# A decoder trunk on one core: the shared values by seven products of halves, with weight sums and a copy of the input through DRAM

## The chip, the core and the metric

The kernel runs on one core of a Trainium2 chip. The core has a matrix engine (TensorE, in profiles PE, with its weight loads as PEld), a vector engine (VectorE, DVE), an activation engine (ScalarE, ACT), a general engine (GpSimd, POOL) and a synchronisation engine (SyncE, SP) which here only issues DMAs. Sixteen DMA engines move data between DRAM and the on-chip memory (SBUF); matmul results go to eight banks of 128 x 512 float32 (PSUM). The metric is the device time of one execution in microseconds (us), taken as the median of the runs.

## The reference

A trunk of two layers on x of 512 tokens by 1024 features, in float32. Layer 0 has a dilated window attention and a gated ConvFFN. After it, keys, values and forget gates are computed once from the residual stream; layer 1 has an attention that uses them, and its own ConvFFN. The part that matters here:

```python
if l == N_A:
    kvf = rms_norm(h, kv_norm) @ w_kvf                  # (512 x 1024) @ (1024 x 2064)
    k_sh = kvf[..., :B_WIDTH].reshape(B, T, B_HEADS, HEAD_DIM)
    v_sh = kvf[..., B_WIDTH:2 * B_WIDTH].reshape(B, T, B_HEADS, HEAD_DIM)
    log_f = jax.nn.log_sigmoid((kvf[..., 2 * B_WIDTH:] + b_f).astype(jnp.float32))
    c_sh = jnp.cumsum(log_f, axis=1)
mix = fox_mixer(rms_norm(h, g[0]), w_q_b[j], w_o_b[j], k_sh, v_sh, c_sh)
```

The values are X W with X of 512 x 1024 (tokens by features, normed and scaled by the key gain) and W the columns 1024 to 2047 of `w_kvf`. The queries use the same normed rows with another gain.

## The kernel before

Every float32 matrix is split into a high and a low part of the matmul's type, and each product takes three matmuls (`mm3`, L294 to L297): high by high, high by low, low by high. A weight of 128 x 1024 is a piece of the list `pieces`. The class `Weights` (L33) loads pieces in the order of the list (`load`, L44: an SP DMA into a `t4` tile), splits them (`high`, L52: ACT casts the high part; `low`, L71: DVE subtracts it and leaves the low part; `high_added` with `low_added`, L92 to L102: ACT also writes the negative, and a DMA issued by POOL adds the raw weight to it) and hands them out (`get`). `high` of piece n first loads up to piece n + 2. The instructions of each engine run in the order in which the program issues them; the engines wait for one another by data and by tile slots. There are 16 slots of 8 KB a partition (`t8`: split weights, input parts, keys, values), 10 of 4 KB (`t4`: raw weights, rows, bias, down-weight sums), 8 of 2 KB (`t2`) and 8 PSUM banks. A new tile takes the slot of one that was released, and its first write waits for the last use of that one.

The stage around the change comes between the two layers. `SharedBoundary` (L485) norms the four token blocks of 128 in the order 2, 3, 0, 1 and transposes them: `transpose` (L512) turns a block on TensorE, DVE multiplies by the key gain (`xf`, L523), ACT and DVE split it into `xkh` and `xkl` (L528, L529), and ACT keeps the unscaled copy in SBUF (`nT`, L533), from which `second` (L535) later makes the queries' input, one 128-feature row of tiles at a time (`xqh` on ACT, L539, `xql` on DVE, L540).

Then, in the order of the program: the first half of the values (columns 1024 to 1535) block by block, with the transposes of blocks 0 and 1 between them; eight key columns (`keys`, L1581: 24 matmuls of width 512, an ACT copy and a DVE subtraction each), with two rows of the queries' input behind each of the first four and one step of the forget gates (`gates`, L1592) behind keys 1 to 5; the second half of the values in four steps over all four blocks, with the first query's product between; and then the attention of layer 1, a loop over 8 pairs of heads and 4 query blocks whose softmax (`f_exp`, L1770) needs DVE, ACT, a bias loaded by SP and a mask by POOL. Each half of the values is 96 matmuls of 128 x 512.

`down_sums` (L602) goes beside it. The ConvFFN's down-projection already uses seven products, and this generator prepares the sums of its weights for layer 1, six pairs here: SP loads a pair into two `t4` tiles, four DVE subtractions (L628) form the sums one step later, and POOL stores them to DRAM (L610). Its seven steps are spread: one before the keys, two behind keys 0 and 1, four behind the steps of the second half of the values. After the values the program has 18 matmuls of query 1, the split of query 2's weight, 12 matmuls of the first scores, and the attention loop.

Of the kernel before, what the change touches and what calls it, by code (L numbers as in the profile page):

```python
# [115 lines left out]
def trunk_kernel(ctx, tc, x, norm_gains, w_qkv_a, w_o_a, w_q_b, w_o_b, kv_norm, w_kvf, b_f,  # L116
# [11 lines left out]
    def t8(shape, dt=F32, name="t8"):  # L128
        return p8.tile(shape, dt, tag="t8", name=name)
# [16 lines left out]
    def cols(w, k0, nk, c0, nc_):  # L146
        return w[k0 * 128:(k0 + nk) * 128, c0:c0 + nc_].rearrange("(k p) c -> p k c", p=128)
# [4 lines left out]
    def add(f):  # L152
        pieces.append(f)
# [19 lines left out]
    def add_cols(w, c):  # L173
        add(lambda raw, c=c: [(raw.rearrange("p (k c) -> p k c", k=8), cols(w, 0, 8, c, 128))])
# [19 lines left out]

    add_rows(w_o_a[0], range(6))
    add_ffn(0)
    for hf in range(2):
        for s in range(4):
            add(lambda raw, hf=hf, s=s: [(raw.rearrange("p (k c) -> p k c", k=2),
                                          cols(w_kvf, 2 * s, 2, 1024 + hf * 512, 512))])  # L200
            if hf == 1 and s == 0:
                add_cols(w_q_b[0], 0)
        if hf == 0:
            for c in range(8):
                add_cols(w_kvf, c * 128)
    for c in range(1, 8):
        add_cols(w_q_b[0], c * 128)
    add_rows(w_o_b[0], range(8))
# [276 lines left out]
    class SharedBoundary(Boundary):  # L485
# [26 lines left out]
        def transpose(self, b, later=None):  # L512
            if self.xT is None:
                self.xT = new_xT(self.name)
                self.nT = [t8([128, 4, T], name=f"nT{i}") for i in range(2)]
            xn, s = self.xn.pop(b), slice(b * 128, b * 128 + 128)
            pts, xfs = [], []
            for i in range(2):
                pt = bank([128, 4, 128], name="xt_ps")
                for k in range(4):  # L520
                    pe.transpose(pt[:, k, :], xn[:, (4 * i + k) * 128:(4 * i + k + 1) * 128], ident)
                xf = t2([128, 4, 128], name="xf")
                dve.tensor_tensor(xf, pt, self.gains[:, 4 * i:4 * i + 4, None].to_broadcast([128, 4, 128]), ALU.mult)  # L523
                pts.append(pt)
                xfs.append(xf)
            for i, xf in enumerate(xfs):
                hi, lo = self.xT[0][i][:, :, s], self.xT[1][i][:, :, s]
                act.copy(hi, xf)  # L528
                dve.tensor_tensor(lo, xf, hi.bitcast(F32), ALU.subtract)  # L529
            if later is not None:  # L530
                later()
            for i, pt in enumerate(pts):
                act.copy(self.nT[i][:, :, s], pt)  # L533

        def second(self, xT, kc):  # L535

            n, g = self.nT[kc // 4][:, kc % 4, :], self.gains[:, 8 + kc:9 + kc]
# [101 lines left out]
    def in_two():  # L639
        return [t4([128, 1024], name="dsums") for _ in range(2)]  # L640
# [937 lines left out]

    kst = {}

    def keys(c):  # L1581
        o = bank([128, T], name="k_ps")
        feat_mm(W.get(), bd2.xT, o, ALL)
# [3 lines left out]
        act.copy(k[:, 0], o)  # L1587
        dve.tensor_tensor(k[:, 1], o, k[:, 0].bitcast(F32), ALU.subtract)

    c8 = t2([16, T], name="c8")  # L1590

# [32 lines left out]
        yield  # L1624


    Vt = {}

    def values(banks, w, s, blocks):
        for b in blocks:  # L1630
            for k in range(2):
                kc = 2 * s + k
                ah, al = xs(bd2.xT, kc, slice(b * 128, b * 128 + 128))
                mm3(banks[b], ah, al, w[0][:, k, :], w[1][:, k, :], kc == 0, kc == KD - 1)

    def value_weight():
        return [t.rearrange("p (k c) -> p k c", k=2) for t in W.get()]

    def keep_values(hf, b, o):
        if hf not in Vt:  # L1640
            Vt[hf] = t8([128, 4, 512], name=f"Vt{hf}")
        (act.copy if b % 2 else dve.tensor_copy)(Vt[hf][:, b, :], o)

    down1 = down_sums([(1, j) for j in range(6)], in_two, pool, 1, 0)
    first, second = bd2.order[:2], bd2.order[2:]
    gate = gates()
    banks = {b: bank([128, 512], name="v_ps") for b in bd2.order}
    wv = []
    W.ahead = 1
    for sp_, b in [(sp_, b) for b in bd2.order for sp_ in (0, 2)]:  # L1650
        if len(wv) < 4:
            wv += [value_weight(), value_weight()]
        for s in (sp_, sp_ + 1):
            values(banks, wv[s], s, (b,))
        if (sp_, b) == (0, first[1]):
            bd2.transpose(second[0], lambda: bd2.norm(second[1]))
        if (sp_, b) == (0, second[0]):
            bd2.transpose(second[1])
            W.ahead = 3
        if b in second:  # L1660
            W.split(min(W.n_split + 1, W.n_get + W.ahead))
            if sp_ == 2:
                for bb in (first[second.index(b)], b):
                    keep_values(0, bb, banks[bb])
    del wv
    next(down1)

    bia = {}

    def load_bias(n):  # L1670
# [34 lines left out]


    xTq = [], []
    for c in range(8):
        keys(c)
        for kc in range(2 * c, min(2 * c + 2, KD)):  # L1710
            if kc % 4 == 0:
                for part, name in zip(xTq, ("xqh", "xql")):
                    part.append(t8([128, 4, T], F32R, name=f"{name}{kc // 4}"))
            bd2.second(xTq, kc)
        if 1 <= c <= 5:
            next(gate)
        if c in (0, 1):
            next(down1)
        if c == 6:
# [6 lines left out]
    banks = [bank([128, 512], name="v_ps") for _ in range(4)]  # L1726
    for s in range(4):
        values(banks, value_weight(), s, range(4))
        next(down1, None)
        if s == 0:  # L1730
            W.ahead = 2
            q_part(0, 0)
            q_part(0, 1)
            load_bias(0)
        elif s == 1:
            q_part(0, 2)
            load_bias(1)
        elif s == 2:
            q_part(0, 3)
            q_high(0)  # L1740
            q_low(0)
            load_bias(2)
    for b in range(4):
        keep_values(1, b, banks[b])


    prob = {}
# [212 lines left out]
```

## Time and profile before

| | us |
|---|---|
| median of 3 runs (1090.96 to 1092.12) | 1091.28 |
| profiled execution, its own time | 1093.78 |
| its span | 1092.0 |
| first half of the values | 509.9 to 533.3 |
| keys and gates | 533.3 to 580.7 |
| second half of the values, with query 0 | 580.7 to 607.9, and a part of query 1 behind it to 612.1 |

The profile is of one execution. Times of the lower rows are counted from the span's start. A group of instructions is given with its line, engine, operation, output and inputs, its count and its mean duration; a timeline row gives start and duration, and in brackets the idle time before it with what ended it. Matmuls are pipelined, so that one lasts longer than the distance to the next.

### The profile page before, as it was taken

To read this page: it belongs to the slowest core of one execution; us is meant where nothing else is said; L and a number is where in the kernel's file an instruction comes from. 1 tells how busy PE (TensorE), PEld (TensorE's weight loads), DVE (VectorE), ACT (ScalarE), POOL (GpSimd) and SP (SyncE) were. 2 spreads that over 40 slices of the span, in tenths; PEclk is the share of its full clock that TensorE was granted. 3 is DMA by queue.
4 is the path that set the end of the run, shared out by engine and by line. 5 is a ranking of instruction groups with operands and counts; after the bars stand their busy time and mean duration, and the time that the engine had idled before them with its cause. 6 is when DMAs were issued, how large, how long until landed. Compare 5 with 4: busy or idle time off the path is not lost.

```text
span 1092.0 us, 18966 instructions
## 1 busy us (share of the span) xinstructions
PE 1080.9 (99%) x6897; PEld 956.8 (88%) x6897; DVE 890.7 (82%) x1450; ACT 694.5 (64%) x1147; POOL 312.0 (29%) x330
## 2 busy tenths in 40 slices
PE   9999999999999999999999999999999999999997
PEld 7888889899999987888888888789899999987886
DVE  4898978679899889997686667868678899889995
ACT  6745666766775756576551587756667677746573
POOL 2643000364665532000001212000355565531000
PEclk9999999999999999999999999999999999999999
DMA  9799855898789978893447757774898878977972
GB/s 288 232 363 412 346 145 151 176 222 215 205 200 225 257 248 280 293 343 97 152 135 254 266 170 205 245 240 130 171 229 192 229 194 206 247 267 257 342 251 77
DMA packets 161525, 250.05 MB, mean 229 GB/s; under 512 B 13088, under 2 KB 106648, under 8 KB 161432
## 3 DMA queue, kind: packets, MB, share of 16 engines
q1 hardware_dynamic: 143784, 189.33, 52.2%
q0 software_dynamic: 16960, 59.52, 24.7%
q8 instruction: 54, 0.88, 0.3%
q14 instruction: 39, 0.32, 0.1%
q10 hardware_dynamic: 688, 0.01, 0.0%
HBM read 172.37 MB, written 39.73 MB: 194 GB/s over the span
## 4 chain that ended last, share of the span: by engine, by line
PE 88%; DMA 3%; DVE 3%; issue 2%; ACT 2%; SPq 1%; POOL 0%; DVEq 0%; ACTq 0%; POOLq 0%
PE up L297 12%; PE up L295 12%; PE up L296 12%; PE acc L297 8%; PE acc L295 8%; PE acc L296 8%; PE v_ps L295 2%; PE v_ps L296 2%; PE v_ps L297 2%; DVE w L831 2%; PE pT_ps L1801 1%; PE first L295 1%; PE qk_ps L295 1%; PE first L296 1%; PE first L297 1%
## 5 line engine op out<-in xcount | busy, mean ns | idle before, releaser
L295 PE MATMUL up<-xsh,w 128*128 128x256 f32 x512 | 144.9, 283 | 0.0
L296 PE MATMUL up<-xsl,w 128*128 128x256 f32 x512 | 144.9, 283 | 0.0
L297 PE MATMUL up<-xsh,w 128*128 128x256 f32 x512 | 144.9, 283 | 0.0
L736 ACT CAST w<-wraw 128x1024 fp32r<-128x1024 f32 x94 | 95.3, 1042 | 65.1 <-DVE wraw L764 44.8
L664 DVE SCALAR_TENSOR_TENSOR bb<-up,conv,bb 128x511 f32<-128x511 f32 (+1 forms) x160 | 118.3, 746 | 19.6 <-ACT bb L670 16.2
L297 PE MATMUL acc<-w 128*128 128x512 f32 (+1 forms) x311 | 120.6, 388 | 1.6 <-DVE w L831 1.6
L295 PE MATMUL acc<-w 128*128 128x512 f32 (+1 forms) x311 | 120.7, 388 | 0.5 <-DVE bb L664 0.5
L686 POOL TENSOR_TENSOR hc<-bb 128x512 f32<-128x512 f32 x44 | 77.8, 1768 | 90.5 <-DVE bb L664 60.2
L296 PE MATMUL acc<-w 128*128 128x512 f32 (+1 forms) x267 | 103.3, 387 | 0.0
L295 PEld LDWEIGHTS up<-xsh,w 128*128 128x128 f32 x512 | 98.3, 192 | 0.0
L296 PEld LDWEIGHTS up<-xsl,w 128*128 128x128 f32 x512 | 98.3, 192 | 0.0
L297 PEld LDWEIGHTS up<-xsh,w 128*128 128x128 f32 x512 | 98.3, 192 | 0.0
L296 PE MATMUL up<-xcl,w 128*128 128x256 f32 (+1 forms) x256 | 79.3, 310 | 0.0
L296 PE MATMUL up<-xbl,w 128*128 128x256 f32 (+1 forms) x256 | 79.3, 310 | 0.0
L295 PE MATMUL up<-xbh,w 128*128 128x256 f32 (+1 forms) x256 | 79.2, 310 | 0.0
L295 PE MATMUL up<-xch,w 128*128 128x256 f32 (+1 forms) x256 | 79.2, 310 | 0.0
L297 PE MATMUL up<-xbh,w 128*128 128x256 f32 (+1 forms) x256 | 79.2, 310 | 0.0
L297 PE MATMUL up<-xch,w 128*128 128x256 f32 (+1 forms) x256 | 79.2, 310 | 0.0
L76 DVE TENSOR_TENSOR w<-wraw,w 128x1024 fp32r<-128x1024 f32 x50 | 60.1, 1221 | 17.6 <-ACT w L58 13.3
L58 ACT CAST w<-wraw 128x1024 fp32r<-128x1024 f32 x61 | 62.7, 1057 | 17.9 <-DMA dsums<-in_w_down_dram 6.9
L297 PEld LDWEIGHTS acc<-w 128*128 128x128 f32 x311 | 58.4, 188 | 14.4 <-DVE w L831 2.5
L295 PEld LDWEIGHTS acc<-w 128*128 128x128 f32 x311 | 58.4, 188 | 12.8 <-ACT bb L689 0.9
(312 smaller groups left out, 3171.6 us busy)
## 6 DMA issues: line engine op xcount, KB each, us to landing
wraw<-in_w_up_dram SPq DMA_DIRECT2D x88, 512.0 KB
w<-wraw POOLq DMA_DIRECT2D x62, 512.0 KB, 5.1
dT<-dsums SPq DMA_DIRECT2D x28, 512.0 KB
dsums<-in_w_down_dram SPq DMA_DIRECT2D x22, 512.0 KB
dsums<-in_w_down_dram SPq DMA_DIRECT2D x44, 256.0 KB
hD<-hc POOLq DMA_DIRECT2D x44, 256.0 KB, 6.1
dact<-hD SPq DMA_DIRECT2D x44, 256.0 KB
wraw<-dT SPq DMA_DIRECT2D x22, 512.0 KB
```

Source lines behind the costliest of these rows:

```text
L58: (copy or self.nc.scalar.copy)(pair[:, 0], raw)
L76: self.nc.vector.tensor_tensor(pair[:, 1], raw, pair[:, 0].bitcast(F32), ALU.subtract)
L295: pe.matmul(o, ah, bh, start=first, stop=False, skip_group_check=shared)
L296: pe.matmul(o, ah, bl, start=False, stop=False, skip_group_check=shared)
L297: pe.matmul(o, al, bh, start=False, stop=last, skip_group_check=shared)
L664: dve.scalar_tensor_tensor(bb[:, s, n:], ps[:, :T - n], cp[:, 2 - n, ch:ch + 1], bb[:, s, n:], ALU.mult, ALU.add)
L686: pool.tensor_tensor(hc[c], bb[:, 0, :], bb[:, 1, :], ALU.mult)
L736: act.copy(w[a][:, 0], raw)
L831: dve.tensor_tensor(w[:, 1], r, w[:, 0].bitcast(F32), ALU.subtract)
L1801: pe.transpose(o[:, k0 + k, :], p[:, hh, k * 128:(k + 1) * 128], ident)
```

## The change

The values' product is cut into halves of tokens, features and columns. X has quarters x11, x12 (blocks 2 and 3, first and second half of the features) and x21, x22 (blocks 0 and 1); W has W11, W12 (first half of the features, columns 1024 and 1536) and W21, W22. Instead of eight products of 256 x 512 by 512 x 512 there are seven, with sums of quarters of X and of W (`sums`, `value_sums`). The weight sums are formed on DVE during the keys, stored to DRAM (`vT`) by POOL, and come back as pieces 12 to 17, 19 and 20 of the list as counted from the first value weight; the first six of these (`ADDED`) are split with the DMA that adds. Input differences are formed in the kept tiles `X`. Two products (x11 W11 and x12 W21) stand ahead of the keys, the other five behind them. Keys 0 and 1 are computed for blocks 2 and 3 first, then, behind the transposes of block 1, for blocks 0 and 1. The unscaled copy of the input goes to DRAM (`nD`) from POOL and comes back by SP, a row at a time (`load_second`), for the queries' input, which is now made among the last five products. Of the seven steps of `down_sums`, one stands behind the third product, one behind the fourth, and five in a row at the end.

```diff
-    for hf in range(2):
-        for s in range(4):
-            add(lambda raw, hf=hf, s=s: [(raw.rearrange("p (k c) -> p k c", k=2),
-                                          cols(w_kvf, 2 * s, 2, 1024 + hf * 512, 512))])
-            if hf == 1 and s == 0:
-                add_cols(w_q_b[0], 0)
...
+    V_BLOCKS = (1024, 0), (1536, 0), (1024, 4), (1536, 4)
...
+    vT = tc.dram_tile([4, 2, 128, 1024], F32, name="vT")
...
+    add_values(0)
+    add_values(2)
+    for c in range(8):
+        add_cols(w_kvf, c * 128)
+    ADDED = set(range(len(pieces), len(pieces) + 6))
+    for n in (2, 0, 3):
+        add_value_sums(n)
+    add_cols(w_q_b[0], 0)
+    add_value_sums(1)
+    add_values(3)
...
-                self.nT = [t8([128, 4, T], name=f"nT{i}") for i in range(2)]
+                self.X = [t8([128, 4, T], name=f"xf{i}") for i in range(2)]
+                self.nD = tc.dram_tile([NB, 2, 128, T], F32, name="nD")
...
-                act.copy(self.nT[i][:, :, s], pt)
+                n = t2([128, T], name="nt")
+                act.copy(n.rearrange("p (k c) -> p k c", k=4), pt)
+                pool.dma_start(self.nD[b, i], n)
+
+        def sums(self):
+            (x11, x12), (x21, x22) = [[self.X[i][:, :, s] for i in range(2)] for s in (HI, LO)]
+            self.S = [[t8([128, 4, T], F32R, name=f"{n}{i}") for n in ("xsh", "xsl")] for i in range(2)]
+            todo = []
+            for o, a, b, n, s in ((x11, x21, x11, 0, HI), (x21, x21, x22, 1, LO), (x22, x22, x11, 0, LO),
+                                  (x12, x12, x22, 1, HI)):
+                dve.tensor_tensor(o, a, b, ALU.subtract)
+                act.copy(self.S[n][0][:, :, s], o)
+                todo.append((n, s, o))
+                yield
+            for n, s, o in sorted(todo, key=lambda e: e[0]):
+                hi, lo = self.S[n]
+                dve.tensor_tensor(lo[:, :, s], o, hi[:, :, s].bitcast(F32), ALU.subtract)
+                yield
...
+    def ahead(n):
+        while W.n_split < W.n_get + n:
+            if W.n_split in ADDED:
+                W.high_added()
+            else:
+                W.high()
+                W.low()
...
+    def value_sums():
+        for p in range(2):
+            (a, b), (c, d) = in_two(), in_two()
+            for n, t in enumerate((a, b, c, d)):
+                sp.dma_start(two_rows(t), value_block(n, p))
+            yield
+            dve.tensor_tensor(d, b, d, ALU.add)
+            dve.tensor_tensor(b, a, b, ALU.add)
+            yield
+            dve.tensor_tensor(a, a, d, ALU.add)
+            dve.tensor_tensor(c, c, a, ALU.add)
+            for n, t in ((3, d), (1, b), (0, a), (2, c)):
+                pool.dma_start(vT[n, p], t)
+            yield
...
+    one_block(v1[0], 0, 0)
+    act.copy(s1[:, 0], v1[0])
+    W.split(W.n_split + 1)
+    one_block(v11[0], 0, 1)
+    one_block(v1[1], 1, 0)
+    bd2.transpose(second[0], lambda: bd2.norm(second[1]))
+    act.copy(s1[:, 1], v1[1])
+    one_block(v11[1], 1, 1)
...
+    kw, kb = [W.get() for _ in range(2)], two_banks("k_ps")
+    for c in range(2):
+        feat_mm(kw[c], bd2.xT, kb[c], HI)
+    bd2.transpose(second[1])
+    next(vsums)
+    ahead(2)
+    for c in range(2):
+        feat_mm(kw[c], bd2.xT, kb[c], LO)
+        keep_keys(c, kb[c])
+        next(vsums)
+    next(vsums)
+    xsums = bd2.sums()
+    for c in range(2, 8):
+        next(xsums, None)
         keys(c)
+        next(xsums, None)
+        if c <= 6:
             next(gate)
+        if c <= 3:
+            next(vsums)
...
+    values(v3, parts[1], 0, [take(2) for _ in range(2)])
+    next(down1)
+    values(v2, S[0], 0, [take(2) for _ in range(2)])
+    query_input(0)
...
+    query_input(1)
+    next(down1)
+    values(v4, S[0], 256, [take(2) for _ in range(2)])
+    for kc in (2, 3, 4):
+        query_input(kc)
...
+    q_part(0, 0)
+    load_bias(0)
+    values(v2, S[1], 0, [take(2) for _ in range(2)], False)
+    q_part(0, 1)
...
+    for kc in (5, 6, 7):
+        query_input(kc)
+    load_bias(1)
+    q_part(0, 2)
+    load_bias(2)
+    q_part(0, 3)
+    q_high(0)
+    q_low(0)
+    values(v2, S[1], 256, [take(1) for _ in range(2)], False)
+    for i in range(2):
+        dve.tensor_tensor(Vt[1][:, 2 + i], v2[i], s1[:, i], ALU.subtract)
+    for _ in down1:
+        pass
```

`take(n)` is `W.get()` and then `ahead(n)`; `values` is the loop of one product over its two weights, two blocks and two rows, 24 matmuls of width 512; `query_input` calls `load_second` for the next row and `second` for its own.

More of the change, by code (lines that the diff above doesn't have):

```diff
@@ new lines, in take @@
+    def take(n):
+        w = W.get()
+        ahead(n)
+        return w
+    def value_sums():
+        for p in range(2):
+            (a, b), (c, d) = in_two(), in_two()
[10 more added lines that the diff above has]
+            yield
@@ L1644, in trunk_kernel @@
     down1 = down_sums([(1, j) for j in range(6)], in_two, pool, 1, 0)
+    vsums = value_sums()
     first, second = bd2.order[:2], bd2.order[2:]
     gate = gates()
-    banks = {b: bank([128, 512], name="v_ps") for b in bd2.order}
-    wv = []
     W.ahead = 1
[L1650 to L1664, printed above, removed]
```

122 lines of the change are left out of this document (70 added, 52 removed).

## The prediction

> **What bounds the kernel now.** I read the page's totals first, then the waits of TensorE, then the stretches of the stage that the change touches.
>
> ```profile
> span 1092.0 us, 18966 instructions
> PE 1080.9 (99%) x6897; PEld 956.8 (88%) x6897; DVE 890.7 (82%) x1450; ACT 694.5 (64%) x1147; POOL 312.0 (29%) x330
> PE acc L297 <- DVE w L831: 1.6, 2, 1.1
> PE pT_ps L1801 <- ACT prob L1779: 1.5, 1, 1.5
> 509.90:533.30 23.40, 23.40 (x113) 19.54 (x112) 16.92 (x27) 14.56 (x29) 0.00 (x0) 1.00 0.48 152
> 533.30:580.70 47.40, 47.40 (x210) 38.13 (x209) 35.26 (x48) 20.75 (x28) 2.13 (x4) 1.00 0.38 116
> 580.70:607.90 27.20, 27.20 (x121) 22.53 (x120) 16.31 (x21) 5.77 (x7) 3.67 (x7) 1.00 1.00 350
> ```
>
> TensorE is busy 99% of the span; its two longest groups of waits are 1.6 and 1.5 us (columns: total, times, longest). The last three rows are the first half of the values, the keys, and the second half of the values (columns: length, then busy us of PE, PEld, DVE, ACT, POOL, the granted clock, DMA share, GB/s). TensorE has no hole in any of them, so every matmul removed pays in full as long as no wait appears. But VectorE works 16.92 + 35.26 + 16.31 = 68.5 of these 98.0 us, and in the last one the DMA engines are already at share 1.00 with 350 GB/s. The change spends on exactly these two.
>
> **What TensorE saves.** A matmul's duration overlaps the next one's, so its price is the distance between starts.
>
> ```profile
> L295 PE MATMUL v_ps<-w,xkh x64: 389/389/476, 509.9 to 607.2; 128*128 128x512 f32 x64
> ...
> 574.81 0.39 PE L296 MATMUL k_ps<-xkl,w 128*128 128x512 f32 x1
> ...
> 580.48 0.39 PE L297 MATMUL k_ps<-xkh,w 128*128 128x512 f32 x1
> ...
> 173.25 0.28 PE L295 MATMUL first<-xbh,w 128*128 128x256 f32 x1
> ...
> 176.00 0.28 PE L297 MATMUL first<-xbh,w 128*128 128x256 f32 x1
> ```
>
> Width 512: 26 starts from 574.81 to 580.48, 5.67 / 25 = 0.227 us. Width 256: 24 starts from 173.25 to 176.00, 2.75 / 23 = 0.120 us. Three lines with 64 matmuls each are 192; seven products of 24 are 168, so 24 x 0.227 = **5.4 us** go. Keys 0 and 1 are now taken in two halves: 96 x 0.120 in place of 48 x 0.227, **0.6 back**. Net **-4.8 us**.
>
> **Two waits right after the first products.** In the new order TensorE does four blocks of 12 matmuls and the transposes of block 0 from 509.9 (to 521.7), then the upper half of keys 0 (24 x 0.120, to 524.6), then of key 1.
>
> ```profile
> 518.72 1.29 DVE L523 TENSOR_TENSOR xf<-xt_ps,gcol 128x512 f32<-128x512 f32 x2
> 520.57 1.05 ACT L302 ACTIVATE junk<-h 128x1024 bf16<-128x1024 f32 x1
> 521.95 1.05 ACT L533 COPY nT<-xt_ps 128x512 f32<-128x512 f32 x2
> 527.86 2.95 ACT L58 CAST w<-wraw 128x1024 fp32r<-128x1024 f32 x3
> ...
> L76 DVE TENSOR_TENSOR w<-wraw,w 128x1024 fp32r<-128x1024 f32 x50 | 60.1, 1221 | 17.6 <-ACT w L58 13.3 <-DMA dsums<-in_w_down_dram 3.9
> ...
> 524.42 1.03 PE L521 MATMUL xt_ps<-ident,xn 128*128 128x128 f32 x8
> 526.43 1.29 DVE L529 TENSOR_TENSOR xkl<-xf,xkh 128x512 fp32r<-128x512 f32 x2
> ```
>
> Key 1's weight is split by ACT only after block 0's ACT work. The split of key 0 (1.2 on DVE) now stands ahead of the xf rows of 518.72, so ACT's copies end at 523.0 + 1.2 = 524.2; the copy of a product (0.5), the cast (1.0) and DVE's low part (1.2) bring 526.9. TensorE is there at 524.6 and can do two matmuls (0.2): **+2.1**. Next, block 1 is transposed and the lower halves of keys 0 and 1 follow with nothing between. In the trace the transposes begin at 524.42, 0.8 before the next matmul, and the low part is there at 526.43 + 0.69 = 527.1; values of another block covered this. Now 1.9 us stay open, less one matmul: **+1.8**. Bounds: nothing if ACT is early, 3 each if it is late.
>
> **The keys become a VectorE stage.** Shapes of the new operations have rows:
>
> ```profile
> L761 DVE TENSOR_TENSOR wraw<-wraw 128x1024 f32<-128x1024 f32 x16 | 19.5, 1217 | 0.1
> L1588 DVE TENSOR_TENSOR kst<-k_ps,kst 128x512 fp32r<-128x512 f32 x8 | 5.5, 684 | 9.6 <-ACT kst L1587 9.6
> L628 DVE TENSOR_TENSOR dsums<-dsums 128x512 f32<-128x512 f32 x88 | 62.4, 712 | 3.3 <-DMA dsums<-in_w_down_dram 1.1
> L1615 DVE RECIPROCAL u<-u 16x512 f32<-16x512 f32 x1 | 3.3, 3333 | 0.0
> ```
>
> From the low part of block 1 (533) to that of key 7's weight, DVE has in order: six weights (K2 to K7) x 1.14 = 6.8, five key copies x 0.61 = 3.1, eight sums of value weights x 1.18 = 9.4, four differences of the input x 1.2 = 4.8, three low parts x 1.14 = 3.4, the gates 6.3 (the reciprocal 3.3): 34 us. It can't run closed up: after a difference ACT casts it, then casts a weight, and only then DVE has its low part (about 2.1 idle, for K4 and K5), and the second set of sums needs loads that need slots of the first set's stores; 4 to 7 us, I take 6. So K7 is ready near 533 + 40 = 573. TensorE, starting at 532.2, has 5.8 for the half keys, four whole keys and the gates (16 matmuls), 3.6, before keys 7: 532.2 + 5.8 + 5 x 5.44 + 3.6 = 568.8. Wait **+5** (bounds 0 and 8). Removed here: eight xql operations, moved behind the keys.
>
> **The value products.** Six weight sums lose their DVE low part: ACT casts and negates (2 x 1.0), a DMA adds.
>
> ```profile
> w<-wraw POOLq DMA_DIRECT2D x62, 512.0 KB, 5.1
> dT<-dsums POOLq DMA_DIRECT2D x16, 512.0 KB, 7.9
> ```
>
> That is 2.0 + 5.1 = 7.1 from raw to ready, against 2.2 with DVE. Sixteen large tiles are all taken (xk 4, S 4, kst 4, Vt 1, weights 3) when keys 7 runs, so the third and fourth sums start at its end: 7.1 to 9.1 against 5.4 of matmuls, 2 to 4 us. After these come two ordinary weights (query 0, first sum 1) whose low parts stand on DVE behind query inputs; these wait for the copy of the input that comes back from DRAM, in SP's queue behind two weights and three down-weight loads, each of which may wait for a slot. I take **+11** for all waits here (3 for the first, some 4 each before query 0 and the products of sum 1); bounds 3 and 20. At no cost: the 14 sums out of PSUM of 0.69 each, 9.7 us, for four DVE copies of 0.68, since DVE has 27.2 - 16.3 = 10.9 us free in the last row of the first fence (7 us if it hadn't); and the copy of the input, 2.1 MB out and 2.1 MB in, whose stores POOL issues while it has nothing else and which the DMA share of 0.38 in the keys covers (12 us at 350 GB/s if it didn't; the second rival holds them).
>
> **The tail decides.** Of the seven steps of the down-weight sums, five now stand in one piece behind the last values, and on DVE ahead of the low part of query 2 and of the first softmax.
>
> ```profile
> 605.37 0.69 DVE L628 TENSOR_TENSOR dsums<-dsums 128x512 f32<-128x512 f32 x1
> 608.30 0.69 DVE L628 TENSOR_TENSOR dsums<-dsums 128x512 f32<-128x512 f32 x1 [0.46 <-DMA dsums<-in_w_down_dram]
> 608.91 1.28 DVE L1642 COPY Vt<-v_ps 128x512 f32<-128x512 f32 x2
> 610.11 1.29 DVE L76 TENSOR_TENSOR w<-wraw,w 128x1024 fp32r<-128x1024 f32 x1
> ...
> 612.08 0.98 PE L1767 MATMUL s_ps<-kst,qst 64*128 64x256 f32 x12
> ...
> 598.01 0.46 SPq L620 DMA_DIRECT2D dsums<-in_w_down_dram  x1
> ```
>
> Let t be the last value matmul. TensorE still has 18 matmuls of query 1 (4.1), 12 of scores (0.9) and 6 more (1.4): 6.4 us of cover, then query 2, whose low part is behind the sums; so are, on POOL, the first masks behind the last stores, on SP the next bias behind the last loads, and on ACT the first exponentials, which all wait for the same end. DVE has 0.4 to see the bank, two sums (1.2), 5 pairs x 4 x 0.71 = 14.2, and query 2's low part 1.2: 17.0. With all data there TensorE waits 17.0 - 6.4 = 10.6. They are not there: of ten t4 tiles three are bias, two raw weights, two pair 1; pair 3 needs a slot from pair 1's store, pair 5 one from pair 3's. Pair 1's first tile is ready at t + 3; store 5.1 to 7.9; load (1.5 by 350 GB/s, 10 by issue at 598.01 and the wait that ends at 608.30; I take 4, as little else moves then): pair 3 starts near t + 13.5, its first tile is done 1.4 later; the same again, 10.5: pair 5 at t + 25.4, done 2.8 later, query 2's low part at t + 29.4. Less 6.4: 23. Landings at 5.1 make it 20. I take **+20**, as the load of the first half is under way early; bounds 10.6 and 26.
>
> One rule speaks of these landings. The Trainium skill, DMA: Bandwidth & Descriptors, section "Anatomy of one DMA — SWDGE (gpsimd) path", fits a POOL-issued DMA as 2.0 us plus bytes / 436e3; for 512 KB that gives an estimate of 3.2 us, and the tail would be some 6 us shorter. The rows above, 5.1 and 7.9, don't agree with it, and they decide.
>
> **Sum.** -4.8 + 2.1 + 1.8 + 5 + 11 + 20 = +35.1. The profiled execution took 1093.78 (span 1092.0 and 1.8 around it): 1128.9 there. The median of the runs is 2.5 lower, 1091.28, so I forecast **1126.4 us**.
>
> **Rivals.**
> - *Loads keep up* (chance 0.18): the tail costs DVE's work alone, 10.6, and the values 6: -4.8 + 3.9 + 5 + 6 + 10.6 = +20.7, **1112**. For it: pairs 1 and 2 can be loaded before t. Against: the slots.
> - *DMA holds longer* (0.14): from K7's load to the tail's end go 13 weights and sums of 0.52 MB (6.8), 2.1 MB of input, six pairs in and out (12.6), 0.9 of bias and six adds (3.1): 25.5 MB, 73 us at 350 GB/s, against 75.4 us by the terms above from keys 7 to the tail's end (5.4, five products 27.2, one query 5.4, waits 11, tail 26.4): no room. Values 20, tail 26: -4.8 + 3.9 + 5 + 20 + 26 = +50, **1141**.
> - *The clock falls in the long wait* (0.08). The granted clock is 1.00 in all rows above, but no wait of TensorE is longer than 1.5 us there. If the long wait let it fall to half for the 24 matmuls of one query behind it, 24 x 0.227 = 5.4 us would be added: **1132**. The Trainium skill, TensorE: Matmul & The Clock Gate, section "Part 1: The HAM clock gate", says that after an idle window of about 3.4 us the clock is halved until about 3.4 us of work are done; no run here shows it.
> - *Faster* (0.05): every wait is covered and only the matmuls count: 1091.3 - 4.8 = **1086.5**. It would need DVE to be past the down-weight sums at t + 6.4, that is four of five pairs summed before t. The program order on DVE speaks against it; the mechanism decides at 4.8 us of waits in all.
> - *No change* (0.02): waits between 2.6 and 7.0 us.
>
> The forecast has 0.53. The range, **1103 to 1146**, goes from all lower bounds for waits but a little of the two early ones (-4.8 + 3 + 0 + 3 + 10.6 = +11.8) to the upper ones with a clock loss (-4.8 + 3.9 + 8 + 20 + 26 + 2 = +55). Faster by over 0.2% (2.2 us, about what a measurement of this kernel can tell) 0.05, within it 0.02, slower 0.93.
>
> **What would show it.** 168 v_ps matmuls at 0.227 and 96 k_ps ones of half width; a wait of about 2 us before key 1 and before the lower half of key 0; DVE without holes through the keys and a wait for a weight's low part at keys 6 or 7; waits in the values for adds by DMA and for the low part of query 0; and one wait of 10 to 26 us before query 2, with DVE on dsums and SP waiting for slots. I'm wrong if TensorE has no hole of over 5 us between the last values and the first pT transposes: then DVE or SP went through the pairs earlier than their order lets me think. If the clock column falls below 1.00 behind that wait, the third rival holds.

## The result: slower by 4.5%, with holes at all the places named

The changed kernel takes 1140.49 us (median of 4 runs, 1138.65 to 1142.46), the kernel before 1091.23 (1090.96 to 1092.12): a ratio of 1.045, interval 1.043 to 1.047. The time lies inside the range, on the side that was forecast, 14 us above the forecast. The profiled execution took 1139.7, that is 45.9 more than the 1093.78 of before.

The totals of the changed kernel's page, with its row of the granted clock (40 equal slices, 9 is nine tenths or more):

```profile
span 1137.9 us, 19179 instructions
PE 1089.5 (96%) x6921; PEld 961.2 (84%) x6921; DVE 916.8 (81%) x1476; ACT 709.6 (62%) x1161; POOL 325.2 (29%) x352
...
PEclk9999999999999999999988889999999999999999
```

These totals split the difference without any theory. Before, TensorE was idle for 1092.0 - 1080.9 = 11.1 us; now it is for 1137.9 - 1089.5 = 48.4: 37.3 more. It is also *busy* for 8.6 us more, though the forecast took 4.8 us of matmuls away. So there are two things to find: the holes, and some 13 us by which the remaining matmuls became longer. The clock row shows where to look for the second: four slices, from 569 to 683 us, that are not at 9 (before, all forty are).

The waits of TensorE (columns: total, times, longest; the rows between are of other stages and of 1.2 us at most):

```profile
PE q_ps L317 <- DVE w L76: 21.7, 2, 19.4
PE v_ps L316 <- DMA w<-wraw: 8.6, 3, 3.9
PE k_ps L317 <- DVE w L76: 4.6, 3, 2.8
...
PE v_ps L316 <- DVE w L76: 1.1, 1, 1.1
PE q_ps L316 <- DVE xql L589: 1.1, 2, 0.8
...
PE k_ps L315 <- ACT xkh L550: 1.0, 1, 1.0
...
PE k_ps L315 <- ACT w L58: 0.8, 1, 0.8
PE k_ps L316 <- DVE xkl L551: 0.3, 1, 0.3
```

In order of time these are: 0.8 and 0.8 before the upper halves of key 1; 1.0 and 0.3 before the lower halves; 1.0 before key 6 and 2.8 before key 7; in the values 3.9, 0.8 and 3.9 for adding DMAs, 2.35 for query 0's low part, 1.1 for a low part and 0.8 and 0.3 for the queries' input; and 19.4 before query 2. That is 1.5 + 1.3 + 3.8 + 13.2 + 19.4 = 39.2, where the forecast had 2.1 + 1.8 + 5 + 11 + 20 = 39.9.

The stretches of the stage (columns: length, then busy us of PE, PEld, DVE, ACT, POOL, granted clock, DMA share, GB/s):

```profile
540.00:580.00 40.00, 36.16 (x150) 27.74 (x149) 33.11 (x36) 18.80 (x23) 4.96 (x8) 0.96 0.68 214
580.00:605.00 25.00, 16.43 (x57) 12.36 (x56) 3.46 (x7) 8.16 (x9) 3.45 (x4) 0.84 0.91 235
605.00:633.00 28.00, 23.38 (x87) 17.44 (x86) 22.78 (x30) 13.01 (x16) 1.11 (x2) 0.90 1.02 300
633.00:660.00 27.00, 7.78 (x42) 5.84 (x40) 15.42 (x23) 1.28 (x1) 5.53 (x11) 0.72 0.89 325
660.00:670.00 10.00, 9.86 (x50) 7.72 (x51) 6.66 (x26) 5.45 (x16) 2.83 (x7) 0.74 0.66 185
```

What is busiest changes from stage to stage: VectorE in the keys (33.11 of 40), the DMA engines in the first part of the values (share 0.91 while VectorE has 3.46 of 25), both in their second part (share 1.02, VectorE 22.78 of 28), and in the tail neither alone. VectorE's timeline shows the tail (columns: start, length; in brackets the idle time before and what ended it):

```profile
634.38 6.25 DVE L677 TENSOR_TENSOR dsums<-dsums 128x512 f32<-128x512 f32 x9
644.37 2.15 DVE L677 TENSOR_TENSOR dsums<-dsums 128x512 f32<-128x512 f32 x3 [3.74 <-DMA dsums<-in_w_down_dram]
647.65 2.87 DVE L677 TENSOR_TENSOR dsums<-dsums 128x512 f32<-128x512 f32 x4 [1.14 <-DMA dsums<-in_w_down_dram]
653.39 0.69 DVE L677 TENSOR_TENSOR dsums<-dsums 128x512 f32<-128x512 f32 x1 [2.87 <-DMA dsums<-in_w_down_dram]
655.30 1.42 DVE L677 TENSOR_TENSOR dsums<-dsums 128x512 f32<-128x512 f32 x2 [1.22 <-DMA dsums<-in_w_down_dram]
658.25 0.69 DVE L677 TENSOR_TENSOR dsums<-dsums 128x512 f32<-128x512 f32 x1 [1.54 <-DMA dsums<-in_w_down_dram]
658.86 1.22 DVE L76 TENSOR_TENSOR w<-wraw,w 128x1024 fp32r<-128x1024 f32 x1
```

Twenty subtractions of five pairs, 14.1 us of work with 10.5 of waiting for the pairs' loads in it, and query 2's low part (L76) last. What the longer matmuls are is seen in TensorE's own rows behind this wait:

```profile
660.14 0.80 PE L317 MATMUL q_ps<-xqh,w 128*128 128x512 f32 x1 [19.36 <-DVE w L76]
660.73 0.63 PE L315 MATMUL q_ps<-xqh,w 128*128 128x512 f32 x1
661.16 0.63 PE L316 MATMUL q_ps<-xql,w 128*128 128x512 f32 x1
```

Starts 0.43 us apart in place of 0.227: half the rate. Such runs of matmuls stand behind five of the waits, those of 2.84, 3.89, 3.91, 2.35 and 19.36 us, with 7, 8, 12, 7 and 9 of them; 43 x 0.2 = 8.6 us, an estimate from their starts. The rest of the 13 us goes to the first matmuls behind each wait (0.80 here against 0.39) and to the modelled ends.

### The profile page after: what moved, and what is told of

Read it like the earlier page. It is cut to its first block, busy times and chain, and to the rows that moved or that the text cites. A ratio compares the mean times of both kernels' runs of the same rounds, so it can differ in the third digit from the quotient of the medians.

```text
span 1137.9 us, 19179 instructions
## 1 busy us (share of the span) xinstructions
PE 1089.5 (96%) x6921; PEld 961.2 (84%) x6921; DVE 916.8 (81%) x1476; ACT 709.6 (62%) x1161; POOL 325.2 (29%) x352
## 4 chain that ended last, share of the span: by engine, by line
PE 81%; issue 6%; DVE 5%; DMA 4%; ACT 3%; POOL 0%; SPq 0%; DVEq 0%; POOLq 0%; ACTq 0%
PE up L317 12%; PE up L316 12%; PE up L315 12%; PE acc L317 7%; PE acc L315 7%; PE acc L316 7%; PE qk_ps L1460 2%; PE pT_ps L1920 1%; PE qk_ps L315 1%; PE first L315 1%; PE first L317 1%; PE first L316 1%; PE qk_ps L316 1%; PE qk_ps L317 1%; PE o_ps L1935 1%
## 5 line engine op out<-in xcount | busy, mean ns | idle before, releaser
L785 ACT CAST w<-wraw 128x1024 fp32r<-128x1024 f32 x94 | 95.3, 1042 | 65.1 <-DVE wraw L813 44.8
L58 ACT CAST w<-wraw 128x1024 fp32r<-128x1024 f32 x67 | 69.0, 1056 | 18.5 <-DMA wraw<-in_w_up_dram 6.7
L96 POOL DMA_DIRECT2D w<-wraw x18 | 15.9, 883 | 211.0 <-ACT w L69 193.8
L76 DVE TENSOR_TENSOR w<-wraw,w 128x1024 fp32r<-128x1024 f32 x50 | 60.0, 1222 | 16.9 <-ACT w L58 16.6
L677 DVE TENSOR_TENSOR dsums<-dsums 128x512 f32<-128x512 f32 x88 | 61.9, 708 | 13.6 <-DMA dsums<-in_w_down_dram 11.4
```

The costliest lines, as they stand in the source:

```text
L58: (copy or self.nc.scalar.copy)(pair[:, 0], raw)
L76: self.nc.vector.tensor_tensor(pair[:, 1], raw, pair[:, 0].bitcast(F32), ALU.subtract)
L96: self.nc.gpsimd.dma_start(pair[:, 1], raw, accum_op=ALU.add)
L677: dve.tensor_tensor(o, p, m, ALU.subtract)
L785: act.copy(w[a][:, 0], raw)
```

## The experiments

The theory: four delays of TensorE, each of its own: the order of the early splits, VectorE in the keys, the deliveries in the values, and the sums of the tail, with a clock that falls behind each long wait. The rivals: that the tail is one of order alone; that the seven products themselves make it; that the slow matmuls are a cost of their own everywhere; that the copy of the input costs. "Saved" is against 1140.49; each ratio's interval is some 0.0017 wide to each side, so a difference of two times is uncertain by 2 to 3 us.

**The tail left out.** Pairs 1 to 5 are not formed, and layer 1's down-projection reads layer 0's sums for them, in `add_ffn` and in `load_two`.

```diff
...
-                sp.dma_start(r4, dT[l][j, :, 1536:2048])
+                sp.dma_start(r4, dT[l if not 1 <= j <= 5 else 0][j, :, 1536:2048])
...
-    down1 = down_sums([(1, j) for j in range(6)], in_two, pool, 1, 0)
+    down1 = down_sums([(1, 0)], in_two, pool, 1, 0)
```

> Left out: the down-weight sums of pairs 1 to 5 of layer 1 (their loads, subtractions and stores); layer 1 reads layer 0's sums in their place. Tail theory (the five steps in a row hold DVE, and through the low part of query 2's weight TensorE, for 19.4 us, and the clock is at half for some microseconds behind that): 24 us less than the changed kernel, near 1116. Rival, DMA load in general (the tail only shows what the whole stage lacks, so that another wait takes its place): under 12 us less, and a wait of over 5 us at another place.

Measured: 1117.32 us, ratio 1.0231 (1.021 to 1.0251): 23.2 saved. Its stretch of the tail:

```profile
633.00:660.00 27.00, 27.00 (x197) 21.97 (x196) 18.64 (x62) 15.51 (x44) 2.45 (x6) 1.00 0.43 130
```

TensorE goes from 7.78 to 27.00 of 27.00 us. The waits of the keys and values stay as they were (4.6 for the keys' low parts, 8.0 for adding DMAs), so the tail is a delay of its own, and about half of the loss.

**Three of the five steps moved forward,** behind query inputs 2 to 4, behind 5 to 7, and before the last product.

```diff
     for kc in (2, 3, 4):
         query_input(kc)
+    next(down1)
...
     for kc in (5, 6, 7):
         query_input(kc)
+    next(down1)
...
     q_low(0)
+    next(down1)
```

> Three of the five last steps stand earlier: behind the query inputs 2 to 4, behind the inputs 5 to 7, and ahead of the last product; two stay at the end. Order theory (only the place on DVE counts): the wait at query 2 shrinks to under 6 us and the kernel gains 14 to 18 us, near 1124. Slots and DMA theory (ten tiles and 350 GB/s set the pace of the pairs wherever they stand): the wait at query 2 shrinks, but waits before query 0 and the products of sum 1 grow by half of it; 4 to 10 us gained, near 1133.

Measured: 1137.2 us, ratio 1.0413 (1.0392 to 1.0434): 3.3 saved, a little less than the 4 to 10 of the second theory. Two of its groups of waits and its stretch of the late values:

```profile
PE q_ps L317 <- DVE w L76: 11.3, 3, 8.1
...
PE v_ps L316 <- DVE w L76: 3.9, 1, 3.9
```

```profile
605.00:633.00 28.00, 20.12 (x61) 14.77 (x60) 21.56 (x29) 9.18 (x12) 2.18 (x4) 0.76 1.08 337
```

The long wait shrinks from 19.4 to 8.1, and most of that comes back earlier: TensorE has 20.12 busy us in the late values against 23.38, with the DMA share at 1.08. The rival of order alone, 14 to 18, falls: the values have no room for the moved steps. Which room is short isn't shown. None of VectorE's steps in the values waits for a pair's load; VectorE works without a hole from 607.20 to 624.58, with the moved subtractions (2.87 us) ahead of two low parts, and then waits 2.99 us for a cast by ACT. So VectorE's own order is as good a reason as the full DMA queues.

**The same tail in the kernel before.** Five steps of its down sums are put behind its last values, and the other two, which stood before and among the keys, go into the second half of the values. Nothing else changes.

```diff
-        next(down1, None)
+        if s < 2:
+            next(down1, None)
...
     for b in range(4):
         keep_values(1, b, banks[b])
+    for _ in down1:
+        pass
```

> The kernel before, with only the order of the down-weight sums changed: two of the seven steps in the second half of the values, five in a row behind it. Tail theory: this alone costs 17 to 26 us, near 1112, with one wait of 14 to 20 us before query 2 and a clock below 1.00 behind it. Rival (the tail hurts only beside the other new transfers): under 10 us.

Measured: 1109.33 us, ratio 1.0158 (1.0137 to 1.0178): 17.4 more than before, with one wait to show for it:

```profile
PE q_ps L297 <- DVE w L76: 16.1, 1, 16.1
```

So the tail does not need the seven products. It is the price of where the five steps lie: 17.4 of the 23.2 us appear in the old kernel too.

**The long wait filled.** 82 and then 90 matmuls of old data into an unused bank stand in front of query 2's matmuls, to keep TensorE busy until its low part is ready.

```diff
+        if n == 1:
+            idle = bank([128, T], name="idle")
+            for _ in range(90):
+                pe.matmul(idle, xTq[0][0][:, 0, 0:128], xTq[0][0][:, 0, :], start=True, stop=True)
         if live:
             f_exp(j, i)
```

> 82 matmuls of 128 x 512 on old data, into a bank that nobody reads, are put into the long wait ahead of query 2 (82 x 0.227 = 18.6 us of its 19.4). Clock theory (a wait of TensorE halves its granted clock for what comes behind): the matmuls behind the wait start 0.227 apart and not 0.43, the scores take 2.1 and not 3, the clock of 660 to 670 us is 1.00 and not 0.74, and 2 to 4 us are gained, near 1137.5. Rival (they are slow because operands come late): the starts stay 0.43 apart, no gain.

Measured with 82: 1138.32 us, ratio 1.0425 (1.0407 to 1.0442). They ended too early; a wait remained, and the matmuls behind it were again at half rate:

```profile
660.55 0.53 PE L317 MATMUL q_ps<-xqh,w 128*128 128x512 f32 x1 [1.94 <-DVE w L76]
660.89 0.62 PE L315 MATMUL q_ps<-xqh,w 128*128 128x512 f32 x1
```

This says nothing about the price, since the clock still fell; so it was taken again with 90.

> As e3_fill with 90 matmuls in place of 82 (20.4 us), so that no wait of over 0.5 us is left before query 2; in e3_fill one of 1.94 us was left, and the matmuls behind it started 0.43 apart all the same. Clock theory (a wait of some 2 us is enough to halve the clock): starts 0.227 apart behind the fill, clock of 660 to 670 us at 1.00, about 2 us less than e3_fill for the matmuls, so 1136 to 1137. Rival (slow for another reason, such as operands or the transfers at that time): 0.43 apart still, no gain.

Measured with 90: 1137.8 us, ratio 1.0415 (1.04 to 1.0431): 2.7 saved. Its stretch behind the tail has the clock at 1.00, where the changed kernel had 0.74:

```profile
660.00:670.00 10.00, 9.97 (x64) 7.72 (x63) 7.79 (x30) 6.91 (x21) 2.02 (x5) 1.00 0.73 227
```

The time saved is no larger than its uncertainty; the rate of the matmuls is not in doubt. The clock falls because TensorE waits. What that costs in this place is read from the starts: from the first matmul that needs the low part to the first transposes behind the scores are 4.5 us here (660.95 to 665.44) and 6.9 in the changed kernel (660.14 to 667.04), so 2.4 us. The 90 matmuls ran on past the low part, which was ready at 659.34, 1.6 us before its first use, so the time saved could have been a little larger.

**All the long holes filled,** with 12, 17, 17 and 10 such matmuls more, ahead of key 7, the second and third product, and query 0.

```diff
...
+        if c == 7:
+            busy(12, bd2.xT[0][0])
         keys(c)
...
+    busy(17, bd2.xT[0][1])
     values(v2, S[0], 0, [take(2) for _ in range(2)])
...
+    busy(17, S[0][0])
     values(v4, S[0], 256, [take(2) for _ in range(2)])
...
+    busy(10, S[0][0])
     q_part(0, 0)
...
```

> The changed kernel with matmuls of old data put into the longer holes of TensorE: 12 ahead of key 7, 17 each ahead of the second and the third value product, 10 ahead of query 0, 90 in the long wait. They leave out nothing and add no result. The clock theory: about 32 matmuls behind the first four waits started 0.43 us apart in place of 0.227, 32 x 0.2 = 6.5 us, and the last wait's 2.7 us is known from the run before; with the holes filled the time falls to about 1139.5 - 9 = 1130.5 (1128 to 1133) and the granted clock of the rows from 560 to 680 us is near 1.00. The rival, that the slow matmuls of these places come of the transfers beside them and not of the holes: the time stays near 1137.8, that of the long wait filled alone.

Measured: 1138.88 us, ratio 1.0429 (1.0412 to 1.0447): no gain over the long wait filled alone, though the keys' matmuls did run at full rate. The forecast of 1130.5 fails. First matmul of the stage, a matmul that waited for an adding DMA, and one that waited for a low part, here:

```profile
509.67 0.39 PE L315 MATMUL v_ps<-w,xkh 128*128 128x512 f32 x1
...
595.23 0.79 PE L316 MATMUL v_ps<-w,xsh 128*128 128x512 f32 x1 [4.05 <-DMA w<-wraw]
...
620.37 0.50 PE L316 MATMUL v_ps<-w,xsh 128*128 128x512 f32 x1 [3.11 <-DVE w L76]
```

and the same three in the changed kernel:

```profile
508.94 0.39 PE L315 MATMUL v_ps<-w,xkh 128*128 128x512 f32 x1
...
594.78 0.50 PE L316 MATMUL v_ps<-w,xsh 128*128 128x512 f32 x1 [0.77 <-DMA w<-wraw]
...
619.48 0.51 PE L316 MATMUL v_ps<-w,xsh 128*128 128x512 f32 x1 [1.14 <-DVE w L76]
```

Counted from the stage's first matmul, the two come at 85.56 and 110.70 us here, at 85.84 and 110.54 there: the same times, with waits of 4.05 and 3.11 in place of 0.77 and 1.14. What TensorE gains by the full clock at key 7 (1.6 us) it waits for longer at the next weights: from the stage's first matmul to the first of query 1 are 124.5 us here and 124.6 there. So in the values the *deliveries* set the time, and slow matmuls there fill time that would be lost anyway. The run does not show the values at full clock: the two waits left are again followed by 12 and 7 matmuls at half rate, and the granted clock is 0.86 from 580 to 605 us and 0.94 from 605 to 633. Of the places tried, the clock is a cost of its own behind the tail alone, where no next wait takes it up.

**Low parts by VectorE in the values,** with no adding DMA.

```diff
-    ADDED = set(range(len(pieces), len(pieces) + 6))
+    ADDED = set()
```

> The six weight sums get their low part from DVE instead of from POOL's adding DMA. Latency theory (the 8.6 us of waits of the products on that DMA come from 7 us of latency, and DVE is free there, busy 3.5 of 25 us): those waits go, with the half clock behind two of them, 8 to 13 us gained, near 1130. DVE theory (DVE is the stage's bound, so six more low parts of 1.14 cost what they save): within 3 us of 1140.5.

Measured: 1132.43 us, ratio 1.0369 (1.0351 to 1.0387): 8.1 saved, and the group of waits for adding DMAs is gone. The five products and query 0 take 45.3 us in place of 53.9, 8.6 less. This is net: the wait for query 0's low part grows from 2.35 to 4.05 us, with 1.6 for ACT's cast of the same weight before it, and the long wait from 19.4 to 20.9. From 570 to 612 us the changed kernel's issues had taken (KB each, median us from issue to landing):

```profile
w<-wraw POOLq DMA_DIRECT2D x6, 512.0 KB, 8.1
```

8.1 us in this stretch, against 5.0 to 5.1 in the medians over the whole kernel. VectorE, which the adding DMAs were to relieve, had 3.46 busy us from 580 to 605 us.

**The early order mended:** key 1's weight is split one product earlier, and block 1 is transposed between the two upper halves.

```diff
-    W.split(W.n_split + 1)
+    W.split(W.n_split + 2)
...
-    for c in range(2):
-        feat_mm(kw[c], bd2.xT, kb[c], HI)
+    feat_mm(kw[0], bd2.xT, kb[0], HI)
     bd2.transpose(second[1])
+    feat_mm(kw[1], bd2.xT, kb[1], HI)
```

> Key 1's weight is split together with key 0's, and block 1 is transposed between the upper halves of keys 0 and 1. Theory (the 2.9 us of waits ahead of the keys come from these two orders alone): they go, 2 to 3 us gained there. They are given back if DVE bounds the keys: then the wait for key 6's and key 7's weights grows from 3.8 to 6 us and the time stays within 1 us of 1140.5.

Measured: 1135.47 us, ratio 1.0393 (1.0376 to 1.041): 5.0 saved, where the four waits that go hold 2.9. One of 0.5 us is left. The mechanism holds. By the two traces 3.5 us of the gain lie there: from the stage's first matmul to the end of the keys are 67.2 us in place of 70.7. The rest is within the uncertainty of 2 to 3 us.

**The copy of the input through DRAM, alone in the kernel before.**

```diff
...
-                act.copy(self.nT[i][:, :, s], pt)
+                n = t2([128, T], name="nt")
+                act.copy(n.rearrange("p (k c) -> p k c", k=4), pt)
+                pool.dma_start(self.nD[b, i], n)
...
```

> The kernel before, with only the unscaled copy of the input taken through DRAM. Theory (the copy is covered when it is needed late): within 1.5 us of the kernel before. Rival (its loads, each some 2.5 us in SP's queue by the changed kernel's trace, hold up weights behind them, and ACT and DVE in the keys): 3 to 8 us slower, with waits in the keys.

Measured: 1090.74 us, ratio 0.9985 (0.9976 to 0.9994). By itself it is covered; there it comes back during the keys, whose DMA share rises from 0.38 to 0.60 with no wait of TensorE. In the changed kernel it comes back during the values, with a median of 10.3 us from issue to landing, and VectorE's order makes it matter. A row of ACT and one of VectorE of the changed kernel:

```profile
605.23 1.57 ACT L588 ACTIVATE xqh<-nt,gcol 128x512 fp32r<-128x512 f32 x2 [11.40 <-DMA nt<-nD]
...
605.99 0.75 DVE L589 SCALAR_TENSOR_TENSOR xql<-nt,gcol,xqh 128x512 fp32r<-128x512 f32 x1 [22.04 <-ACT xqh L588]
```

VectorE stands still for 22 us in front of the first query input; behind it in its order wait two sums out of PSUM, a second input, four down sums and only then query 0's low part. The copy was not taken back alone in the changed kernel: the kept tiles hold its slots.

**Three edits together:** no tail, low parts by VectorE, the early order. Layer 1 reads layer 0's sums for pairs 1 to 5.

```diff
+    ADDED = set()
...
+    W.split(W.n_split + 2)
...
+    down1 = down_sums([(1, 0)], in_two, pool, 1, 0)
```

> The changed kernel with three edits at once: the five last steps of the down sums left out (layer 1 reads layer 0's sums for these pairs, so that part of the output is wrong), the low parts by VectorE instead of adding DMAs, and the second key weight split earlier with block 1's transposes between the two upper halves. If the parts add, as they do where each is a wait of TensorE of its own: 1139.5 - 23 - 8 - 5 = 1103.5 (1100 to 1106), and what is left over the kernel before (some 12 us) is the wait of key 7, query 0's low part and the clock behind them. If one part's gain was only shifted by another: over 1108.

Measured: 1105.63 us, ratio 1.0121 (1.0106 to 1.0136): 34.9 saved, where 23.2 + 8.1 + 5.0 = 36.3. The parts add, within 1.4 us. What is left is 13.5 us over the kernel before. A part of it stands in VectorE's rows:

```profile
596.39 2.87 DVE L677 TENSOR_TENSOR dsums<-dsums 128x512 f32<-128x512 f32 x4
599.17 2.35 DVE L76 TENSOR_TENSOR w<-wraw,w 128x1024 fp32r<-128x1024 f32 x2
```

The low part of query 0's weight (L76, the first of the two) comes behind four down sums in this order, and TensorE waits 4.05 us for it, behind 2.34 for ACT's cast of the same weight; key 7 waits 2.84 as before.

**The tail moved behind,** pair 1 as it was, pairs 2 to 5 by one step in three units of attention, into `t8` tiles.

```diff
+    sums1 = down_sums([(1, j) for j in range(2, 6)], in_one, pool, 1, 0)
...
+        if n in (2, 5, 8, 11, 14):
+            next(sums1)
```

> The changed kernel with the down sums of pairs 2 to 5 moved behind the long wait: pair 1 still ends before query 2, and the other four pairs go, one step in three units of attention (units 2, 5, 8, 11, 14), into tiles of the other shape. Nothing is left out. If the long wait is a matter of place only, VectorE (27.85 busy of 40 in the row from 660 to 700 us) has room for five steps of 2.7 us, and the time comes near that without the steps, 1117.3, and some 2 for pair 1: 1119 (1116 to 1123). The rival, that VectorE's steps or their loads hold attention up wherever they lie, 2.7 to 4 us a step: 1130 to 1138.

Measured: 1124.29 us, ratio 1.029 (1.0272 to 1.0307): 16.2 saved, 7 above the kernel without the steps and just outside what was expected. The long wait is gone; the one for query 0's low part is 4.04. Two waits for adding DMAs of attention's weights come in its place (1.14 and 2.14 us), in a stretch that the pairs fill:

```profile
660.00:700.00 40.00, 36.68 (x303) 29.93 (x300) 32.06 (x101) 29.45 (x77) 10.48 (x21) 1.00 0.99 315
```

**The same with the low parts and the early order.**

> The run before with two more edits: low parts by VectorE in place of adding DMAs (8.1 saved alone) and the second key weight split earlier with block 1's transposes between (5.0 saved alone); nothing is left out. The runs so far did not quite add (1105.6 with the steps left out, where 1103.5 was the sum): 1106 to 1110 where the steps are covered, 1120 and more where they are not. The theory that seven products can't pay in this place says that it stays over the kernel before, 1092, by the waits of key 7 and query 0 alone (13 us of holes with the matmuls slowed behind them); the rival is that the moves free VectorE and the DMAs there and it comes under 1095.

Measured: 1110.44 us, ratio 1.0174 (1.0159 to 1.0189): 30.1 saved, and nothing left out; just over the 1106 to 1110 of the covered case. Its largest groups of waits in the stage and in the attention behind it:

```profile
PE q_ps L317 <- DVE w L76: 4.0, 1, 4.0
PE k_ps L317 <- DVE w L76: 3.7, 2, 2.8
PE q_ps L317 <- DMA w<-wraw: 3.4, 2, 2.1
PE v_ps L316 <- DVE w L76: 2.1, 2, 1.3
PE q_ps L315 <- ACT w L58: 1.8, 1, 1.8
```

It is the best complete form of seven products that was run, and it stays 18 us over the kernel before. No version of seven products came under the kernel before.

## Why the prediction held, and where its sum was off

The traces of the two profiled executions split the 45.9 us by stage. Before, the stage starts at 509.9, the second half of the values at 580.7 and query 1 at 607.9, with no holes. In the changed kernel the five products behind the keys and query 1 start here:

```profile
579.67 0.39 PE L315 MATMUL v_ps<-w,xkh 128*128 128x512 f32 x1
...
633.57 0.39 PE L315 MATMUL q_ps<-xqh,w 128*128 128x512 f32 x1
```

| stretch | worked out | late | forecast |
|---|---|---|---|
| first two products and keys | 579.67 - 508.94 = 70.7; before, 70.8 with 48 more value matmuls: 70.8 - 48 x 0.227 + 0.6 = 60.5 | 10.2 | 2.1 + 1.8 + 5 = 8.9 |
| five products and query 0 | 633.57 - 579.67 = 53.9; 144 matmuls x 0.227 = 32.7 | 21.2 | 11 |
| from query 1 to the end | 1137.9 - 633.57 = 504.3; before, 1092.0 - 607.90 = 484.1 | 20.2 | 20 |

With the 4.8 saved and 1.0 less ahead of the stage this makes 45.8. The forecast had +35.1, so on these executions it missed 10.8 us, and nearly all of it is in the value products. The remaining 3 of the 14 us come of the medians: the profiled execution of the kernel before was 2.5 above its median, that of the changed kernel 0.8 below.

- **What the matmuls save (-4.8).** The groups of the changed kernel by shape, one of the three lines of each:

```profile
L315 PE MATMUL v_ps<-w,xsh 128*128 128x512 f32 x32 | 14.7, 459 | 0.0
L315 PE MATMUL v_ps<-w,xkh 128*128 128x512 f32 x24 | 9.4, 393 | 0.0
L315 PE MATMUL k_ps<-xkh,w 128*128 128x256 f32 x32 | 9.3, 289 | 1.8 <-ACT xkh L550 1.0 <-ACT w L58 0.8
```

  3 x (32 + 24) = 168 value products and 3 x 32 = 96 of half width, as counted. The saving can't be seen by itself, since no run had the seven products without holes.
- **Two early waits (+2.1, +1.8).** In their places, 1.5 and 1.3; taking both away saved 5.0.
- **VectorE in the keys (+5).** It waited at keys 6 and 7, with 3.8 us; VectorE has 33.11 of 40 us there. The matmuls behind it at half rate cost nothing more by the end of the values, as the run with all holes filled shows.
- **The value products (+11).** This term was sized too small: 21.2, over its upper bound of 20. Its waits are 13.2; 27 matmuls at half rate, which stand in for more waiting, make 27 x 0.2 = 5.4; the rest goes to the edges of the waits, where a matmul's row lasts 0.39 us though the next could start after 0.227, and where the first two starts are 0.33 to 0.59 apart. The step that failed is "3 for the first": these adding DMAs were priced at 5.1 us, the median over the whole kernel, while the prediction itself had the stage's DMA share at 1.00. They took 8.1, and the three waits for them hold 8.6, which is what the run without them gained there. Of these, 3.89 and 0.77 are for the third and fourth sums, which the prediction reckoned with; 3.91 is for the fifth, for which it had no term. The "some 4 each" before query 0 and the products of sum 1 were 2.35 and 1.1, and the reason given, the copy that comes back late, is what VectorE's 22 us show.
- **At no cost: the copy of the input.** Right where nothing else fills the queues (ratio 0.9985), wrong as a statement about this stage; the term above already held its delay.
- **The tail (+20).** All that follows the values is 20.2 longer; the wait is 19.36. Pair 5's sums start 20.0 us behind the last value matmul (633.35), not 25.4, and end 25.6 behind it, not 28.2. The reckoning gave 23 and took 20, since the load of pair 3's first half would be under way early; the ninth subtraction, pair 3's first, does follow without a hole. Leaving the tail out saves 23.2, of which 2.4 are the clock, by the run with 90 filling matmuls.
- **The clock (rival, 0.08).** As a mechanism it is there, behind every wait of 2.3 us and more in the changed kernel, so its chance was too low. As a price it was too high: 5.4 was given for the long wait, 2.4 was measured, since the rate came back after 4 us. The Trainium skill, TensorE: Matmul & The Clock Gate, section "Part 1: The HAM clock gate", gives an idle window and a busy window of about 3.4 us each. The trace agrees with the second roughly (3.0 to 5.3 us at half rate), not with the first: waits of 1.94, 2.35 and 2.84 us were enough.
- **Loads keep up (0.18), DMA holds longer (0.14).** Between the two: in the tail the loads came somewhat earlier than reckoned, in the values they came later. The second rival's 20 for the values was right, its 26 for the tail was not. That its sum, 1141, is so near the time is partly luck: on the profiled executions it is 4 us too high (50 against 45.9), and the medians hide that.

By the runs the 49 us are: 23 for the tail, 8 for the adding DMAs, 5 for the early order, and 13 that remain, of which the 4.8 saved are already taken off. In the trace with these three edits TensorE is 6.6 us late up to the keys' end (the waits at key 6, 0.87, and key 7, 2.84, with what follows from them) and 12.0 late in the values (2.34 and 4.05 for query 0's weight, 1.9 for two low parts of sums, with what follows). These were located in the traces, not taken away one by one.

## What to carry to other kernels

Before work is taken off an engine that is busy 99% of the time, count what pays for it on the engines beside it stage by stage: 24 matmuls of 0.227 us were bought with weight sums, stores, loads and adding DMAs around a stretch whose DMA share was already 1.00. Price a DMA by its time in the stage where it will run, not by its median over the kernel (8.1 against 5.1 us here). And steps that were spread thinly to be covered are not free to gather: five of them in one piece cost 17 us in the old kernel and 23 in the new.

## What was not expected of the hardware

Waits between 1.9 and 2.9 us went both ways. 1.94 us (the run with 82 filling matmuls), 2.35 and 2.84 us (the changed kernel) were followed by matmuls at half rate; 1.93 and 2.73 us (the run with the early order mended) and 2.14 us (the run with the steps in attention) were not. Those of 3.1 us and more were followed by it each time in the traces of these runs. The ones of 1.2 to 1.5 us in this stage and behind it never were; those of 1.60 and 1.83 tell nothing, as a wait of 4 us follows two matmuls later. So the length of a wait alone doesn't decide, and what else does was not tried. The slow stretch can begin late: behind the wait of 2.35 us, which ended at 612.57, the starts were 0.23 apart for 1.3 us and only then 0.43.

```profile
612.57 0.50 PE L317 MATMUL q_ps<-xqh,w 128*128 128x512 f32 x1 [2.35 <-DVE w L76]
612.90 0.40 PE L315 MATMUL q_ps<-xqh,w 128*128 128x512 f32 x1
...
614.13 0.63 PE L317 MATMUL v_ps<-w,xsl 128*128 128x512 f32 x1
614.55 0.63 PE L315 MATMUL v_ps<-w,xsh 128*128 128x512 f32 x1
```
